# Two-layer hybrid attention trunk: in the grouped-query attention, the weight preparation of the filling matmuls is ordered behind the instructions its engines were given before it

## Chip, cores, metric

The kernel runs on one core of a Trainium2 chip. The metric is the device time of one execution in microseconds, the median of several runs.

## What is computed

A trunk of two layers (`DEPTH = 2`) over 512 latent tokens and 256 context tokens of width 1024, all in fp32. Each layer projects its normalised input once (`w_in`), runs two attentions beside each other (a neighbourhood attention, NA, and a grouped-query attention, GQA), gates each, projects each (`w_o_a`, `w_o_b`), merges them by sigmoid gates and projects the result (`w_out`). The second layer has no context queries (`update_ctx` is false there). What matters here:

```python
    b_att = _gqa_latent(qb, k_all, v_all)      # 8 query heads of 64, 2 key heads, 768 keys
    ...
    o_a = (a_att * jax.nn.silu(a_z)) @ w_o_a   # w_o_a: 512 x 1024
    o_b = (b_att * jax.nn.silu(b_z)) @ w_o_b
    merged = jax.nn.sigmoid(g_a) * o_a + jax.nn.sigmoid(g_b) * o_b
    return merged @ w_out
```

`g_a` and `g_b` are columns of the input projection (1024 each). Their matmuls, and those of `o_a`, do not depend on the GQA and are used to fill TensorE while the attention's softmax runs on the other engines.

## The kernel before

**Weights.** Every large projection is three passes of a matmul on numbers that are split into a high and a low part. `load_w2` brings a chunk of weights, 256 columns, as tiles of 128x512: SyncE issues a DMA into `raw`, ScalarE casts it (`whi`, line 420), and VectorE or GpSimd, tile by tile in turn (`mix_lo`), subtracts (`wlo = raw - whi`, line 422). `raw` has three buffers; `whi` and `wlo` have eight each, which is two chunks of four tiles. A chunk of the gates has four tiles, a chunk of `w_o_a` two.

**Stages of a layer.** Input projection, NA heads, query and key preparation of the GQA, then 8 GQA heads, then merge and output projection. In the GQA stage a list `fill` holds, alternately, the loading of a chunk and the pieces (groups of matmuls) that use a chunk. `in_order` builds it: the loads of the first two chunks, then for each chunk its pieces, followed by the load of the chunk two places further on.

```python
            fill = in_order(gates[n_na:] + o_chunks("a", prepare, evac_a))
            run(fill, 2)
```

So `run(fill, 2)` gives the loads of chunks 0 and 1. Chunks 0 to 4 are what is left of the gates (called A0 to A4 here) and four chunks of `w_o_a` follow (O0 to O3). Some pieces are given ahead of the heads (four in layer 0, two in layer 1); `pipeline` spreads the rest of the list over the 8 heads: first the scores of head h, then the values of head h-1, then a few entries of `fill`. The pieces write one PSUM buffer `psf` (lines 435 to 437, one line a pass); ScalarE empties it for the gates (`zt`, line 625), VectorE for `w_o_a` (`tg`, line 703). Ahead of the first piece of O0 stands `prepare`: `hilo` splits the gated NA output, four casts on ScalarE (`gah`, line 667) and four subtractions on GpSimd (`gal`, line 668).

**A head.** Four times: scores on TensorE into one of two PSUM buffers (`pss`, lines 886 and 887), maximum on VectorE (line 1157), exponential on ScalarE (line 1158, `p`), cast of `p` to half precision on ScalarE (`h`, line 837), its low part on VectorE or GpSimd (line 838), and a transposing DMA. The next head's query is split by a cast (line 879) and a subtraction on VectorE (`qs`, line 880). The values come a head later: a small matmul that brings the sums' reciprocals in place (line 849), the products (lines 1174 and 1175), and `ho` on ScalarE and VectorE (lines 824 and 825). In layer 0 each head also has its context queries (lines 899 to 921).

**What sets the order.** A scheduler with a simulated timeline puts the instructions of each engine into order; the order in which the code gives them counts only where a dependency says so. `behind(engine, fn, after)` adds such dependencies: it calls `fn` and ties what `fn` gives to `engine` in a row behind the instructions `after`. They are program order on that one engine and not a wait on a semaphore. `latest(engine, n)` names the last n instructions given to an engine so far.

Of the kernel before, what the change touches and what calls it, by code (L numbers as in the profile page):

```python
# [38 lines left out]
ON_PE, ON_DVE = mybir.EngineType.PE, mybir.EngineType.DVE  # L39
ON_ACT, ON_POOL, ON_SP = mybir.EngineType.Activation, mybir.EngineType.Pool, mybir.EngineType.SP  # L40
# [32 lines left out]
def hybrid_kernel(es: ExitStack, tc, x, ctx, cvec, w_ada, w_ada0, small, gvec, w_in, w_o_a, w_o_b, w_out,  # L73
# [17 lines left out]
    def big(name):  # L91
        return bigp.tile([128, 3072], F32, tag="big", name=nm(name))
# [319 lines left out]
    def load_w2(src, col0, nk, lo_eng):  # L412

        res = []
        for i in range(nk // 2):
            raw = raw_tile()
            nc.sync.dma_start(raw.rearrange("p (k n) -> p k n", k=2),
                              src[256 * i:256 * i + 256, col0:col0 + 256].rearrange("(k p) n -> p k n", k=2))
            hi = wp.tile([128, 512], F32R, tag="whi", name=nm("whi"), bufs=8)
            S.copy(hi, raw)  # L420
            lo = wp.tile([128, 512], F32R, tag="wlo", name=nm("wlo"), bufs=8)
            lo_eng(i).tensor_tensor(lo, raw, F(hi), ALU.subtract)  # L422
            res += [(hi[:, c:c + 256], lo[:, c:c + 256]) for c in (0, 256)]
        return res
# [27 lines left out]
    def chan_proj(w, f, a, n0, n1, evac, late=0):  # L452


        ps = psw(n1 - n0)
        nk = len(w)
        wh = lambda k, i: w[k][i][:, 128 * f:128 * f + 128]
        act = lambda k, i: R(a(i, k)[:, n0:n1])
        for k in range(late):
            T.matmul(ps, wh(k, 0), act(k, 0), start=k == 0, stop=False)  # L460
            T.matmul(ps, wh(k, 1), act(k, 0), start=False, stop=False)
        for k in range(late):
            T.matmul(ps, wh(k, 0), act(k, 1), start=False, stop=False)
        for k in range(late, nk):
            mm3(ps, (wh(k, 0), wh(k, 1)), (act(k, 0), act(k, 1)), k == 0, k == nk - 1)
        evac(f, n0, n1, ps)
# [3 lines left out]
    def latest(engine, n):  # L470
        return [i.name for i in nc.cur_bb.bb.instructions if i.engine == engine][-n:]

    def behind(engine, fn, after=None):

        n = len(nc.cur_bb.bb.instructions)
        after = latest(engine, 1) if after is None else after
        fn()
        for i in nc.cur_bb.bb.instructions[n:]:
            if i.engine == engine:
                for last in after:  # L480
                    tc.add_manual_dep(i, last, mybir.DependencyInfo(
                        mybir.DependencyClass.NoSync, mybir.DependencyReason.DATA), reason="program order")
                after = [i.name]
# [6 lines left out]
    def run(fill, n):  # L490
        for _ in range(min(n, len(fill))):
            fill.pop(0)()
# [102 lines left out]
    def layer(l, hx, nxt, start):  # L595
# [22 lines left out]
        def fill_chunks(col0, dst, spill, silu, eng):  # L618

            def evac(f, n0, n1, ps):  # L620
                if spill is None:
                    d = dst().rearrange("p (f n) -> p f n", f=4)[:, f, n0:n1]
                else:
                    d = ztp.tile([128, 512], F32, tag="zt", name=nm("zt"))[:, :n1 - n0]
                S.activation(d, ps, AF.Tanh, scale=0.5)  # L625
                if silu:
                    V.scalar_tensor_tensor(d, d, 1.0, ps, ALU.add, ALU.mult)
                if spill is not None:
                    (nc.sync if not first else G if silu else S).dma_start(spill[:, f, n0:n1], d)
            res = []  # L630
            for i in range(2):
                st = {}

                def ld(i=i, st=st):
                    st["w"] = load_w2(W, col0 + 256 * i, KT, eng)
                res.append((ld, [lambda f=f, n0=n0, n1=n1, i=i, st=st:
                                 chan_proj(st["w"], f, a_hx, n0, n1, lambda f, a, b, ps: evac(2 * i + f, a, b, ps))
                                 for f in range(2) for n0, n1 in spans]))
            return res

        def in_order(chunks):

            res = [ld for ld, _ in chunks[:2]]
            for i, (_, pieces) in enumerate(chunks):
                res += pieces
                if i + 2 < len(chunks):
                    res.append(chunks[i + 2][0])
            return res

        tg = [None] * 4  # L650
        n_na = GATES[l]
# [21 lines left out]
        def o_chunks(br, prepare, evac):  # L673

            src = (w_o_a if br == "a" else w_o_b)[l]
            act = lambda part, k: gated[br][part][:, k, :]
            res = []
            for i in range(4):
                st = {}

                def ld(i=i, st=st):
                    st["w"] = load_w2(src, 256 * i, 4, pool_lo if br == "b" and i == 0 else mix_lo)
                pieces = [lambda f=f, n0=n0, n1=n1, i=i, st=st:
                          chan_proj(st["w"], f, act, n0, n1, lambda f, a, b, ps: evac(2 * i + f, a, b, ps),
                                    3 if br == "b" and i == 0 and first else 0)
                          for f in range(2) for n0, n1 in spans]
                res.append((ld, ([prepare] if i == 0 and prepare else []) + pieces))
            return res
# [80 lines left out]
        fill = fill_chunks(C_AZ, lambda: za, None, True, mix_lo) + fill_chunks(C_BZ, None, zs, True, mix_lo)  # L769
        gates = []  # L770
        for c in range(4):
            gates += g_chunks(c)
        fill = in_order(fill + gates[:n_na])
        run(fill, 2)
        for t in range(qt):
# [11 lines left out]
        if True:  # L787
# [326 lines left out]
                run(bg, 1)  # L1114
            hp["lag"] = 2
            qbv = big("qb").rearrange("p (j n) -> p j n", j=4)
            fill = in_order(gates[n_na:] + o_chunks("a", prepare, evac_a))
            run(fill, 2)

            def evac_bq(t, ps):  # L1120
# [83 lines left out]
        with tc.tile_pool(name=f"mrg{l}", bufs=1, reuse_waits="tile") as mp:  # L1204
# [16 lines left out]
            chunks = o_chunks("b", None, evac_b)  # L1221
# [223 lines left out]
    def nxt():  # L1445
        if not hx1:
            hx1.extend([[big("hx") for _ in range(2)] for _ in range(2)])
        return hx1
    layer(0, hx0, nxt, start)
    layer(1, hx1, None, None)  # L1450


# [73 lines left out]
```

## Time and profile before

| | |
|---|---|
| time, median of 3 runs | 1111.2 us (1111.06 to 1111.54) |
| the profiled execution | 1110.55 us, span 1108.8 us |
| mean granted clock of TensorE | 0.995 |
| TensorE matmul busy | 1074.5 us (97%) |
| VectorE busy | 767.4 us (69%) |
| ScalarE busy | 617.2 us (56%) |
| GpSimd busy | 470.1 us (42%) |

Times in the profile are from the start of the span. The GQA stage of layer 0 lies at about 375 to 530 us, that of layer 1 at about 920 to 1040 us. In the rows, a number in brackets at the end is the idle time of the engine just before the instruction, with what ended it. PE is TensorE, DVE VectorE, ACT ScalarE, POOL GpSimd, SPq the DMA queue of SyncE.

### The profile page before, as it was taken

The numbers are of one execution on the slowest core, as the hardware profiler recorded it, in microseconds if no ns is written. First come the engines' busy times: TensorE is split into PE (matmuls) and PEld (weight loads), VectorE is DVE, ScalarE is ACT, GpSimd is POOL, SyncE is SP. The second block draws the span as 40 slices with busy tenths as digits, with TensorE's granted clock in tenths as the row PEclk, the third lists the DMA queues.
The fourth block names the chain that finished last, engine by engine and source line by source line (L and its number), as shares of the span: only waits on it lengthen the run. The fifth ranks groups of instructions, "written<-read, shape, count | busy, mean of one in ns | idle before, by whom it ended". The sixth has DMA issues, their size and how long they took to land. (4 is left out here: it accounts for less than half of the span.)

```text
span 1108.8 us, 16943 instructions
## 1 busy us (share of the span) xinstructions
PE 1074.5 (97%) x5672; PEld 876.9 (79%) x5672; DVE 767.4 (69%) x1600; ACT 617.2 (56%) x1236; POOL 470.1 (42%) x397
## 2 busy tenths in 40 slices
PE   8999999899999999979999999999999999999998
PEld 6688888788888877757788878888877888777677
DVE  5567799974378478676577785466997665777473
ACT  6464279776333566655330275444899446786430
POOL 1044235554256244454521455232355472564531
PEclk9999999999999999989999999999999999999999
DMA  9454325554543498769533542453565536879642
GB/s 374 153 169 143 91 70 116 125 137 121 174 141 117 132 205 185 172 185 271 171 105 125 166 136 82 138 165 99 132 148 130 156 106 171 200 232 236 188 152 77
DMA packets 236001, 171.79 MB, mean 155 GB/s; under 512 B 160141, under 2 KB 201865, under 8 KB 234249
## 3 DMA queue, kind: packets, MB, share of 16 engines
q1 hardware_dynamic: 228576, 156.31, 51.7%
q0 software_dynamic: 2368, 7.87, 2.2%
q10 hardware_dynamic: 4968, 6.53, 1.8%
q8 instruction: 45, 0.74, 0.3%
q14 instruction: 44, 0.35, 0.1%
HBM read 115.58 MB, written 17.32 MB: 120 GB/s over the span
## 5 line engine op out<-in xcount | busy, mean ns | idle before, releaser
L838 POOL TENSOR_TENSOR h<-p,h 128x256 f16<-128x256 f32 (+2 forms) x104 | 113.1, 1096 | 167.7 <-ACT h L837 119.9
L422 POOL TENSOR_TENSOR wlo<-raw,whi 128x512 fp32r<-128x512 f32 x70 | 98.8, 1416 | 124.5 <-ACT whi L420 80.9
L435 PE MATMUL psf<-hx,whi 128*128 128x512 f32 (+1 forms) x360 | 137.5, 382 | 2.5 <-ACT zt L625 1.3
L437 PE MATMUL psf<-hx,wlo 128*128 128x512 f32 (+1 forms) x360 | 135.5, 376 | 0.0
L436 PE MATMUL psf<-hx,whi 128*128 128x512 f32 (+1 forms) x360 | 135.4, 376 | 0.0
L435 PE MATMUL psx<-whi,hx 128*128 128x512 f32 (+1 forms) x328 | 121.0, 372 | 0.0
L420 ACT CAST whi<-raw 128x512 fp32r<-128x512 f32 x136 | 82.9, 620 | 67.5 <-DMA raw<-in_w_in_dram 48.3
L437 PE MATMUL psx<-whi,hx 128*128 128x512 f32 (+1 forms) x328 | 120.0, 367 | 0.0
L436 PE MATMUL psx<-wlo,hx 128*128 128x512 f32 (+1 forms) x328 | 119.6, 366 | 0.0
L408 POOL TENSOR_TENSOR wlo<-raw,whi 128x512 fp32r<-128x512 f32 x40 | 59.5, 1489 | 119.2 <-ACT whi L405 76.0
L405 ACT CAST whi<-raw 128x512 fp32r<-128x512 f32 x88 | 54.2, 623 | 96.8 <-PE psx L437 34.2
L508 POOL TENSOR_TENSOR ss<-ss,ehalf 128x8 f32<-128x8 f32 (+2 forms) x40 | 63.6, 1593 | 77.8 <-DVE ss L505 72.5
L422 DVE TENSOR_TENSOR wlo<-raw,whi 128x512 fp32r<-128x512 f32 x66 | 70.8, 1073 | 35.2 <-ACT whi L420 34.1
L837 ACT CAST h<-p 128x256 f16<-128x256 f32 (+2 forms) x136 | 81.6, 616 | 7.7 <-DMA ct<-h 3.7
L435 PEld LDWEIGHTS psf<-hx,whi 128*128 128x128 f32 x360 | 67.8, 188 | 15.1 <-ACT zt L625 2.5
L1157 DVE CUSTOM_DVE_ANT_0 p<-pss,vb 128x768 f32<-128x768 f32 x64 | 60.4, 954 | 25.4 <-PE pss L887 22.7
L1158 ACT ACTIVATE p<-pss,mx 128x768 f32<-128x768 f32 x64 | 57.6, 901 | 35.7 <-DVE mx L1157 34.8
L437 PEld LDWEIGHTS psf<-hx,wlo 128*128 128x128 f32 x360 | 67.8, 188 | 11.8
L436 PEld LDWEIGHTS psf<-hx,whi 128*128 128x128 f32 x360 | 67.9, 189 | 10.7
L437 PEld LDWEIGHTS psx<-whi,hx 128*128 128x128 f32 x328 | 61.9, 189 | 10.2
L436 PEld LDWEIGHTS psx<-wlo,hx 128*128 128x128 f32 x328 | 62.0, 189 | 9.4
L435 PEld LDWEIGHTS psx<-whi,hx 128*128 128x128 f32 x328 | 61.8, 189 | 9.1 <-issue 0.2
(338 smaller groups left out, 2972.4 us busy)
## 6 DMA issues: line engine op xcount, KB each, us to landing
raw<-in_w_in_dram SPq DMA_DIRECT2D x168, 256.0 KB, 2.9
rawb<-in_w_ada_dram SPq DMA_DIRECT2D x48, 256.0 KB, 2.8
raw<-in_w_out_dram SPq DMA_DIRECT2D x32, 256.0 KB, 2.9
tg<-gs SPq DMA_DIRECT2D x4, 1536.0 KB, 7.1
rawx<-in_w_ada_dram SPq DMA_DIRECT2D x4, 1024.0 KB, 10.7
rawy<-in_w_ada_dram SPq DMA_DIRECT2D x4, 1024.0 KB, 9.3
gs<-zt ACTq DMA_DIRECT2D x16, 256.0 KB, 2.9
raw<-in_w_o_a_dram SPq DMA_DIRECT2D x16, 256.0 KB, 3.1
```

Source lines behind the costliest of these rows:

```text
L405: S.copy(hi[:, :n], raw[:, :n])
L408: e.tensor_tensor(lo[:, :n], raw[:, :n], F(hi[:, :n]), ALU.subtract)
L420: S.copy(hi, raw)
L422: lo_eng(i).tensor_tensor(lo, raw, F(hi), ALU.subtract)
L435: T.matmul(ps, lhs[0], rhs[0], start=first, stop=False)
L436: T.matmul(ps, lhs[0], rhs[1], start=False, stop=False)
L437: T.matmul(ps, lhs[1], rhs[0], start=False, stop=last)
L508: G.tensor_tensor(ss, ss, ehalf[:, :n], ALU.pow)
L837: S.copy(h[:, 0], p[:, :n])
L838: eng.tensor_tensor(h[:, 1], p[:, :n], h[:, 0], ALU.subtract)
L1157: V.tensor_tensor_reduce(p, pss, lift, -1.0, 3e38, ALU.add, ALU.min, mx[:, 0:1])
L1158: S.activation(p, pss, AF.Exp, bias=mx[:, 0:1], accum_out=r[:, i:i + 1])
```

## The change

`in_order` takes a flag. Where it is set, which is only for the list `fill` of the GQA stage (of both layers), the loads of the chunks after the first two (A2, A3, A4, O0 to O3) are given through `tied`: their casts on ScalarE stand in a row behind the last four instructions given to ScalarE before them, and their subtractions on VectorE in a row behind the last four given to VectorE. Their DMAs and the subtractions on GpSimd get no such dependency. No instruction is added or removed.

```diff
-        def in_order(chunks):
+        def tied(fn):
+            behind(ON_ACT, lambda: behind(ON_DVE, fn, latest(ON_DVE, 4)), latest(ON_ACT, 4))
+
+        def in_order(chunks, tie=False):
 
             res = [ld for ld, _ in chunks[:2]]
             for i, (_, pieces) in enumerate(chunks):
                 res += pieces
                 if i + 2 < len(chunks):
-                    res.append(chunks[i + 2][0])
+                    ld = chunks[i + 2][0]
+                    res.append((lambda ld=ld: tied(ld)) if tie else ld)
             return res
...
-            fill = in_order(gates[n_na:] + o_chunks("a", prepare, evac_a))
+            fill = in_order(gates[n_na:] + o_chunks("a", prepare, evac_a), True)
             run(fill, 2)
```

What this does to the engines' rows is shown at two places. In the changed kernel the line numbers behind the edit are four higher (line 1158 is 1162 there). The numbers behind a name are those of the tiles, the same in both kernels.

The first place is the start of layer 1's heads. On ScalarE before, from the third exponential of head 0 (`p_9883`) to the second of head 1 (`p_10007`); the casts of chunk A2 (`whi_9906`, `whi_9912`, `whi_9918`, `whi_9924`) stand some 15 rows above, before head 0's first exponential:

```order
L420 CAST whi_10085<-raw_10083 128x512
L625 ACTIVATE zt_9981<-psf_9956 128x512
L879 CAST qs_10145<-qb_9536 64x512
L1158 ACTIVATE p_9883,r_2006_9851<-pss_9878,mx_9884 128x768
L837 CAST h_9887<-p_9883 128x768
L1158 ACTIVATE p_9896,r_2006_9851<-pss_9891,mx_9897 128x768
L837 CAST h_9900<-p_9896 128x768
L625 ACTIVATE zt_10114<-psf_10089 128x512
L1158 ACTIVATE p_9994,r_2041_9988<-pss_9989,mx_9995 128x768
L1158 ACTIVATE p_10007,r_2041_9988<-pss_10002,mx_10008 128x768
```

And ScalarE now:

```order
L625 ACTIVATE zt_9981<-psf_9956 128x512
L883 CAST qs_10145<-qb_9536 64x512
L1162 ACTIVATE p_9883,r_2006_9851<-pss_9878,mx_9884 128x768
L1162 ACTIVATE p_9896,r_2006_9851<-pss_9891,mx_9897 128x768
L841 CAST h_9887<-p_9883 128x768
L841 CAST h_9900<-p_9896 128x768
L420 CAST whi_9906<-raw_9904 128x512
L420 CAST whi_9912<-raw_9910 128x512
L420 CAST whi_9918<-raw_9916 128x512
L1162 ACTIVATE p_9994,r_2041_9988<-pss_9989,mx_9995 128x768
L1162 ACTIVATE p_10007,r_2041_9988<-pss_10002,mx_10008 128x768
```

Three casts of A2 have moved from ahead of head 0 to the end of it, and the fourth comes still later; the cast `whi_10085`, of chunk A3, has left this place too.

On TensorE, in the same place before, the last score of head 0 (`pss_9891`) is followed by the 24 matmuls of A2's first piece (`psf_10089`), of which the first six are:

```order
L887 MATMUL pss_9891<-gk_9240,qs_9847 128x256
L435 MATMUL psf_10089<-hx_6680,whi_9906 128x512
L436 MATMUL psf_10089<-hx_6682,whi_9906 128x512
L437 MATMUL psf_10089<-hx_6680,wlo_9908 128x512
L435 MATMUL psf_10089<-hx_6680,whi_9906 128x512
L436 MATMUL psf_10089<-hx_6682,whi_9906 128x512
L437 MATMUL psf_10089<-hx_6680,wlo_9908 128x512
```

And TensorE now, from the second score of head 1 (`pss_10002`):

```order
L890 MATMUL pss_10002<-gk_9240,qs_9984 128x512
L891 MATMUL pss_10002<-gk_9240,qs_9984 128x512
L890 MATMUL pss_10002<-gk_9240,qs_9984 128x256
L891 MATMUL pss_10002<-gk_9240,qs_9984 128x256
L853 MATMUL pst_10041<-ident,r_2006_9851 128x128 x4
L435 MATMUL psf_10089<-hx_6680,whi_9906 128x512
L436 MATMUL psf_10089<-hx_6682,whi_9906 128x512
L890 MATMUL pss_10015<-gk_9240,qs_9984 128x512
L891 MATMUL pss_10015<-gk_9240,qs_9984 128x512
L890 MATMUL pss_10015<-gk_9240,qs_9984 128x256
L891 MATMUL pss_10015<-gk_9240,qs_9984 128x256
L437 MATMUL psf_10089<-hx_6680,wlo_9908 128x512
```

The piece has moved behind the first two scores of head 1 (`pss_9989`, `pss_10002`) and the small matmul of head 0's divisor (`pst_10041`), and the third score (`pss_10015`) cuts it after two matmuls.

The second place is in layer 0, where `prepare` runs. On VectorE before, around the low part of the second tile of chunk O1 (`wlo_5499`):

```order
L1157 ISA p_5553,mx_5554<-pss_5548,vb_3419 128x768
L1157 ISA mx_5554 128x1
L850 SCALAR_TENSOR_TENSOR zb_4067<-pst_5616,vb_3419,zb_4067 64x512
L422 TENSOR_TENSOR wlo_5499<-raw_5495,whi_5497 128x512
L880 TENSOR_TENSOR qs_5721<-qb_3734,qs_5721 64x768
L847 RECIPROCAL r_5431<-r_5431 128x2
L825 TENSOR_TENSOR ho_5471<-psv_5462,ho_5471 64x256
```

And VectorE now:

```order
L1161 ISA p_5553,mx_5554<-pss_5548,vb_3419 128x768
L1161 ISA mx_5554 128x1
L854 SCALAR_TENSOR_TENSOR zb_4067<-pst_5616,vb_3419,zb_4067 64x512
L884 TENSOR_TENSOR qs_5721<-qb_3734,qs_5721 64x768
L851 RECIPROCAL r_5431<-r_5431 128x2
L829 TENSOR_TENSOR ho_5471<-psv_5462,ho_5471 64x256
```

`wlo_5499` has left the row and comes some time later; the split of the next head's query (`qs_5721`) takes its place, and the rest of the row is as before.

On GpSimd before, in the same stretch, where `gal_5309` is the four subtractions of `prepare`, `wlo_5493` the first tile of O1 and `wlo_5671` the first of O2:

```order
L829 TENSOR_TENSOR zb_4067<-zb_4067,ho_5458 64x512
L422 TENSOR_TENSOR wlo_5493<-raw_5489,whi_5491 128x512
L668 TENSOR_TENSOR gal_5309<-za_1053,gah_5308 128x768 x4
L422 TENSOR_TENSOR wlo_5671<-raw_5667,whi_5669 128x512
L829 TENSOR_TENSOR zb_4067<-zb_4067,ho_5471 64x256
```

And GpSimd now:

```order
L833 TENSOR_TENSOR zb_4067<-zb_4067,ho_5458 64x512
L672 TENSOR_TENSOR gal_5309<-za_1053,gah_5308 128x768 x4
L833 TENSOR_TENSOR zb_4067<-zb_4067,ho_5471 64x256
L842 TENSOR_TENSOR h_5434<-p_5430,h_5434 128x512
L422 TENSOR_TENSOR wlo_5493<-raw_5489,whi_5491 128x512
```

The four subtractions of `prepare` now stand between two additions to `zb`, and the low parts of O1 and O2 that stood around them come later.

## Prediction

> **What bounds the kernel now.** I read the page first, then the busy time by stage, then the waits of the matmul engine stage by stage, then the timeline around its longest wait.
>
> ```profile
> span 1108.8 us, 16943 instructions
> PE 1074.5 (97%) x5672; PEld 876.9 (79%) x5672; DVE 767.4 (69%) x1600; ACT 617.2 (56%) x1236; POOL 470.1 (42%) x397
> ```
>
> TensorE is busy for 97% of the span, so no other engine's work is the bound as such. The change adds no work; it can only open or close holes on TensorE, or change its clock. The busy time in the layer-0 heads, the layer-1 heads and the rest (columns: length, then busy time and instruction count for PE, PEld, DVE, ACT and POOL, then granted clock) shows where holes are:
>
> ```profile
> 375.00:530.00 155.00, 141.33 (x786) 113.36 (x784) 111.04 (x198) 101.04 (x195) 72.25 (x51) 0.97 0.81 196
> 920.00:1040.00 120.00, 116.60 (x550) 88.74 (x550) 81.43 (x130) 83.70 (x150) 64.70 (x43) 1.00 0.86 213
> ```
>
> The heads of layer 0 have 155.00 - 141.33 = 13.7 us of idle TensorE and a clock under 1; those of layer 1 have only 3.4 us. The waits of TensorE name them (the first two rows are of layer 0's window, the third of layer 1's):
>
> ```profile
> PE psv L849 <- DVE ho L825: 5.8, 1, 5.8
> PE psf L435 <- ACT zt L625: 2.0, 2, 1.6
> PE psf L436 <- POOL gbl L668: 1.1, 1, 1.1
> ```
>
> So there is one large hole in layer 0 to win, and in layer 1 a stage that is nearly full, where a cast that comes late can only cost.
>
> **Part 1: layer 0, where `prepare` runs.** The hole in detail:
>
> ```profile
> 482.17 1.14 ACT L420 CAST whi<-raw 128x512 fp32r<-128x512 f32 x2
> 483.33 0.38 ACT L625 ACTIVATE zt<-psf 128x256 f32<-128x256 f32 x1
> 483.76 0.49 PE L435 MATMUL psf<-gah,whi 128*128 128x512 f32 x1 [1.60 <-ACT zt L625]
> 484.84 0.79 PE L436 MATMUL psf<-gal,whi 128*128 128x512 f32 x1 [0.58 <-POOL gal L668]
> 493.56 0.69 PE L849 MATMUL psv<-ident,r 128*128 128x128 f32 x2 [5.79 <-DVE ho L825]
> ...
> 481.75 1.27 POOL L422 TENSOR_TENSOR wlo<-raw,whi 128x512 fp32r<-128x512 f32 x1
> 482.98 7.12 POOL L668 TENSOR_TENSOR gal<-za,gah 128x768 fp32r<-128x768 f32 x4
> 490.05 1.27 POOL L422 TENSOR_TENSOR wlo<-raw,whi 128x512 fp32r<-128x512 f32 x1
> ...
> 483.66 8.22 DVE L422 TENSOR_TENSOR wlo<-raw,whi 128x512 fp32r<-128x512 f32 x1
> 491.91 0.95 DVE L880 TENSOR_TENSOR qs<-qb,qs 64x768 fp32r<-64x768 f32 x1
> 492.89 0.17 DVE L847 RECIPROCAL r<-r 128x2 f32<-128x2 f32 x1
> 493.09 0.42 DVE L825 TENSOR_TENSOR ho<-psv,ho 64x256 f32<-64x256 f32 x1
> ```
>
> VectorE's subtraction `wlo_5499` starts at 483.66, while GpSimd runs the four `gal` and then another `wlo` without a break, and ends at 491.88, 0.56 us after GpSimd's last. Behind it on VectorE stand the split of the query, the reciprocal and `ho`, and TensorE waits for that `ho`. The clock falls too (granted clock is the third column from the end):
>
> ```profile
> 484.00:488.00 4.00, 3.18 (x8) 2.15 (x7) 4.00 (x1) 3.92 (x10) 4.00 (x3) 0.59 1.07 421
> 492.00:496.00 4.00, 2.44 (x8) 2.15 (x9) 3.13 (x5) 0.00 (x0) 1.84 (x2) 0.50 0.08 18
> 496.00:500.00 4.00, 4.00 (x15) 2.85 (x15) 2.44 (x5) 1.82 (x3) 0.37 (x1) 0.71 0.68 163
> ```
>
> In the last of these windows half rate holds for (1 - 0.71) x 2 x 4.00 = 2.3 us, so until about 498.3; from 493.56 on, 4.7 us run at half rate and some 2.4 us are lost to it. Price of the whole incident: 1.60 + 0.58 + 5.79 + 2.4 = 10.4 us.
>
> What the change removes here: the two casts at 482.17, so `zt` at 483.33 can follow the matmuls at once and the 1.60 hole nearly goes; the `wlo` of GpSimd at 481.75, so `gal` starts 1.23 us sooner; the `wlo` behind `gal`; and `wlo_5499` itself. What stays: the split of the query, which also reads two operands from SBUF, now arrives at VectorE at 483.66, in the middle of `gal`. I take it that it is held as `wlo_5499` was: until 482.98 + 7.12 - 1.23 = 488.87, plus the 0.56 above and its follow-up (0.17 + 0.42 and the gaps, 493.56 - 492.86 = 0.70), which puts the matmul of line 849 at about 490.4 instead of 493.56. The hole on TensorE is still there, so the half clock is too. Gain 3.1 us. Bounds: 1.2 us if VectorE is held as much longer as before, 10.4 less 0.9 (the query's own 0.95) = 9.5 us if it is not held at all.
>
> **Part 2: layer 1, start of the heads.** Here the move costs:
>
> ```profile
> 931.14 0.62 ACT L420 CAST whi<-raw 128x512 fp32r<-128x512 f32 x1 [0.86 <-DMA raw<-in_w_in_dram]
> 932.66 0.90 ACT L1158 ACTIVATE p<-pss,mx 128x768 f32<-128x768 f32 x1
> 933.46 0.19 ACT L1158 ACTIVATION_READ_ACCUMULATOR p<-pss,mx 128x1 f32 x1
> 935.44 0.83 ACT L837 CAST h<-p 128x768 f16<-128x768 f32 x1
> ...
> 936.35 1.65 POOL L838 TENSOR_TENSOR h<-p,h 128x768 f16<-128x768 f32 x1 [3.50 <-ACT h L837]
> ...
> 931.25 0.96 DVE L1157 CUSTOM_DVE_ANT_0 p<-pss,vb 128x768 f32<-128x768 f32 x1 [1.16 <-PE pss L887]
> ...
> 931.64 0.28 PE L887 MATMUL pss<-gk,qs 128*128 128x256 f32 x1
> 932.31 0.50 PE L435 MATMUL psf<-hx,whi 128*128 128x512 f32 x1 [0.39 <-ACT zt L625]
> 937.89 0.39 PE L886 MATMUL pss<-gk,qs 128*128 128x512 f32 x1
> 938.60 0.39 PE L886 MATMUL pss<-gk,qs 128*128 128x512 f32 x1
> 939.30 0.60 PE L849 MATMUL pst<-ident,r 128*128 128x128 f32 x4
> ```
>
> Before, TensorE filled 932.31 to 937.89 (5.58 us, 24 matmuls of A2's first piece), while ScalarE did head 0's last exponentials and casts. Now the piece's casts come behind all of that. Step by step:
>
> - The maximum at 931.25 ends at 932.21, so `p_9883` runs 932.25 to 933.3 (0.90 and the sum's 0.19), some 0.4 us sooner than before, as the cast at 931.14 is gone from ScalarE. Both score buffers are full until then: `pss_9989` starts at 933.3, TensorE idle from 931.92.
> - `p_9896` ends at 934.35; then `pss_10002` (one score is 938.60 - 937.89 = 0.71) until 935.06, and the divisor's matmul, about 0.35.
> - The two casts `h` (0.83 each) end at 936.0 and `whi_9906` (0.62) at 936.6: two matmuls, then TensorE waits again. `whi_9912` and `whi_9918` (0.57 each by the row at 482.17) go ahead of `p_9994`, which ends at 938.8; then `pss_10015` runs until 939.5. The piece's low part `wlo_9908` on GpSimd, behind the 1.65 of `h_9900` and with some 1.3 of its own (the row at 481.75), is there by 939.0.
> - At 939.5 there remain 22 of the 24 matmuls, 5.1 us, so this stretch of work ends at 944.6. Before, all but the 0.71 of `pss_10015` was done at 939.65: 940.35. Loss 4.2 us. Bounds 3.5 (if `zt` and the query's cast let ScalarE start sooner) and 4.8 (if the exponential starts at 932.66 as before).
>
> TensorE has about 2.2 us of work in the 6.9 us to 938.8 (two scores, the divisor's, two of the piece). In layer 0 a stretch so thin brought half clock: the row 484 to 488 has 0.59, that is 4.00 x (1 - 0.59) = 1.64 us lost. I add 1.7 for one such stretch here; bounds 0 and 3.3 (two). [...]
>
> Nothing makes this up later: the whole stage has 3.4 us of idle TensorE, in pieces of other causes. SyncE's queue also changes: the load of A2's fourth tile and of two tiles of A3 now stand between the transposes of head 0 and head 1, waiting for `raw` buffers that the late low parts free at about 940; head 1's transposes come after that anyway (its first exponential ends at 938.8). Cost nothing; cover gone would be about 1 us on the values of head 1, a head later.
>
> **Part 3: everywhere else.** In layer 0 the same shift hits a start of the heads where the context queries and a finished piece stand in between; by the casts' durations (4 x 0.62) against that cover I count 0, at most 0.7. Later chunks arrive one head later and are used one head later: 0. At the end of layer 1 casts of `w_o_b`'s part stand ahead of the last exponentials; of before's holes there (1.1 in the row above) one may close, and up to three casts and three `gbh` may delay the last values (about 6 x 0.57 less cover = 2.7): I take +0.5.
>
> **Sum.** -3.1 + 4.2 + 1.7 + 0.5 = +3.3 us on the profiled 1110.55: 1113.85. The median of the runs, 1111.2, is 0.65 above the profiled run, so 1114.5.
>
> **Rivals.** *VectorE slips in between (faster).* In layer 1 the same four subtractions hold VectorE only for one of them:
>
> ```profile
> 984.31 5.63 POOL L668 TENSOR_TENSOR gal<-za,gah 128x512 fp32r<-128x512 f32 x4 [0.51 <-ACT gah L667]
> 987.38 1.42 DVE L422 TENSOR_TENSOR wlo<-raw,whi 128x512 fp32r<-128x512 f32 x1
> ```
>
> If the query's split gets in so, `ho` is there before TensorE asks for it, the clock stays full, and part 1 gains 9.5: -9.5 + 4.2 + 1.7 + 0.5 = -3.1, or 1108.1 as a median. It decides from a wait of under 2 us at 483.66. Against it: 8.22 us over four `gal`, in this very place. [...] Chance 0.25.
>
> *No thin stretch (no change).* The clock in layer 1 stays full and the tail is even: -3.1 + 4.2 = +1.1, 1112.3. For it: the stretch still has some matmuls in it every 2 us. Chance 0.17.
>
> *The hole of layer 0 stays (slower, more).* GpSimd's row behind `gal` keeps VectorE out as long as before, and the gain is 1.2 at most; with two slow stretches in layer 1: -1.2 + 4.2 + 3.3 + 0.5 = +6.8, 1118.0. For it: VectorE got in only when GpSimd's whole row had run out. Chance 0.15.
>
> That the change moves nothing is excluded by the order of the instructions, which differs at both places.
>
> **How the numbers follow.** The forecast has the rest, 0.43: 1114.5, its own range 1112 to 1117. A measurement of this kernel can tell about 0.2%, 2.2 us, from no change, so up to 1113.4 is the same: some 0.08 of the forecast and 0.14 of the second rival, 0.22. Slower: 0.35 of the forecast, 0.15 and 0.03: 0.53. Faster: 0.25. The range takes in the first rival with 1.1 us to spare and the last with 1.5: 1107.0 to 1119.5.
>
> **What would show it.** Right: in layer 0 the wait of line 853 (849 before) for `ho` shrinks to about 2.5 to 3.5 us, with the split of the query at about 6 us in place of the 8.22; in layer 1 waits on `p` and `whi` of together about 4.5 us between 931 and 940, and a clock under 1 right after. Wrong: no long VectorE instruction beside `gal` (first rival), a clock of 1.00 from 936 to 944 (second), or VectorE held past 491 (third); or waits over 1 us at places that part 3 counts at 0.

## The result and the profile after

| | before | after |
|---|---|---|
| median | 1111.2 us (5 runs, 1109.65 to 1111.54) | 1124.44 us (5 runs, 1123.44 to 1127.78) |
| ratio | | 1.0127, 95% interval 1.0115 to 1.0139 |
| profiled execution, span | 1110.55, 1108.8 us | 1125.78, 1123.9 us |

The change makes the kernel 1.3% slower, 13 us, outside the range that was given. The traces compared below differ by 15.1 us of span, some 2 us more than the medians. The head of the page after:

```profile
span 1123.9 us, 16910 instructions
PE 1078.6 (96%) x5672; PEld 880.5 (78%) x5672; DVE 769.5 (68%) x1600; ACT 617.3 (55%) x1236; POOL 466.2 (41%) x397
```

The same 5672 matmuls take 4.1 us longer (1078.6 to 1074.5; the mean granted clock is 0.989 after and 0.995 before), and TensorE idles 45.3 us instead of 34.3. Of the 15.1 us of span, 11.0 are holes and 4.1 slower matmuls. Where in the program they arise is read from the same work's start in the two traces. Two pairs of rows, before and after each: the first transposes of layer 1's input (line 343, the same in both kernels) and the first scores of layer 1's NA heads (line 974, after 978); the two times are the first and the last start:

```profile
L343 PE MATMUL pst<-ident,y x48: 270/272/327, 639.2 to 672.1; 128*128 128x128 f32 x48
L974 PE MATMUL pss<-kh,qs x24: 387/392/481, 775.2 to 847.6; 128*128 128x512 f32 x24
```

```profile
L343 PE MATMUL pst<-ident,y x48: 269/273/330, 646.6 to 687.8; 128*128 128x128 f32 x48
L978 PE MATMUL pss<-kh,qs x24: 386/392/480, 787.3 to 859.3; 128*128 128x512 f32 x24
```

By the first transposes of layer 1, where layer 0 ends, the changed kernel is 7.4 us late; by the NA heads of layer 1 it is 12.1. The last score of GQA head 0 in layer 1 ends at 931.92 before and 943.75 after, 11.8 late, and the span's end is 15.1 late: the GQA stage of layer 1 and what follows cost only 3.3.

Layer 0's GQA stage, before and after (columns as in the prediction: length, busy time of PE, PEld, DVE, ACT, POOL, then granted clock):

```profile
480.00:504.00 24.00, 15.98 (x72) 11.86 (x70) 19.20 (x21) 12.62 (x25) 14.81 (x11) 0.79 0.76 242
504.00:550.00 46.00, 44.10 (x242) 34.18 (x243) 27.45 (x46) 21.16 (x42) 25.66 (x19) 1.00 0.76 191
```

```profile
480.00:504.00 24.00, 15.65 (x72) 11.27 (x71) 19.84 (x22) 12.51 (x24) 13.66 (x10) 0.79 0.77 237
504.00:550.00 46.00, 37.57 (x188) 29.63 (x187) 24.57 (x40) 18.89 (x38) 24.10 (x19) 0.89 0.86 221
```

The stretch with `prepare` is as bad as before; nothing was won there. The stretch behind it, which the prediction counted at nothing, lost 6.5 us of TensorE's busy time (44.10 to 37.57), and what ran there ran at a clock of 0.89.

The hole at `prepare`, after; TensorE, VectorE and GpSimd:

```profile
482.55 0.50 PE L436 MATMUL psf<-gal,whi 128*128 128x512 f32 x1 [0.89 <-POOL gal L672]
488.92 0.79 PE L890 MATMUL pss<-gk,qs 128*128 128x512 f32 x1 [5.42 <-ACT p L909]
491.16 0.69 PE L853 MATMUL psv<-ident,r 128*128 128x128 f32 x2 [0.59 <-DVE ho L829]
497.23 0.50 PE L890 MATMUL pss<-gk,qs 128*128 128x512 f32 x1 [1.42 <-ACT p L1162]
...
480.27 7.54 DVE L905 TENSOR_SCALAR mx<-mx 128x2 f32<-128x2 f32 x1
489.50 0.95 DVE L884 TENSOR_TENSOR qs<-qb,qs 64x768 fp32r<-64x768 f32 x1
...
480.69 7.10 POOL L672 TENSOR_TENSOR gal<-za,gah 128x768 fp32r<-128x768 f32 x4
```

The held instruction is neither a low part nor the query's split. It is the addition of a constant to a maximum of 128x2 numbers (line 905), which takes 0.15 to 0.38 us at its seven other places and 7.54 here, to the end of the four `gal`. It stands ahead of the next score's maximum, so TensorE stops at a score, 4 us sooner than before. A sign of this stood in the trace of before, at the same instruction, and the prediction passed over it (the GpSimd addition to `zb` beside it ran from 480.50 to 481.79, so both ended nearly together):

```profile
481.32 0.56 DVE L901 TENSOR_SCALAR mx<-mx 128x2 f32<-128x2 f32 x1
```

The holes behind it, after, and SyncE's queue at that place, before and after:

```profile
512.41 0.38 PE L1178 MATMUL pst<-ht,vb 128*128 128x512 f16 x1 [2.31 <-issue]
521.55 0.65 PE L853 MATMUL pst<-ident,r 128*128 128x128 f32 x4 [1.83 <-DVE r L851]
540.08 0.58 PE L435 MATMUL psf<-gah,whi 128*128 128x256 f32 x1 [3.21 <-DVE tg L707]
...
537.47 1.83 DVE L422 TENSOR_TENSOR wlo<-raw,whi 128x512 fp32r<-128x512 f32 x1 [1.68 <-ACT whi L420]
```

```profile
498.35 0.96 SPq L671 DMA_DIRECT2D tg<-gs  x2
499.75 6.02 SPq L842 DMA_TRANSPOSE ct<-h  x1
```

```profile
498.53 0.47 SPq L675 DMA_DIRECT2D tg<-gs  x1
499.86 10.32 SPq L846 DMA_TRANSPOSE ht<-h  x3
512.73 0.71 SPq L675 DMA_DIRECT2D tg<-gs  x1
```

Loads of `tg` of 1.5 MB stand before the transposes of a head's probabilities in both kernels. After, the products of a head (line 1178) come 13 us behind the last head's (499.47 and 512.41), as fewer of `w_o_a`'s pieces stand between; before, 21 us (499.27 and 520.51). The row at 512.41 names no releaser, but the view of the transposed tiles `ht` from 496 to 516 does: TensorE's matmul waits 2.3 us for them, and they take up to 9.6 us from issue to landing (minimum, median and maximum below; before, 3.3, 3.8 and 4.2, with no wait of TensorE):

```profile
PE pst L1178: 2.3, 1
DMA to landing us min/median/max: 3.6/8.0/9.6
```

The largest hole, 3.21 at 540.08, is of another kind. TensorE waits for `tg`, the emptying of `psf` on VectorE, and this stands behind the low part at 537.47, which waited for its cast and then ran 1.83 us beside GpSimd's `gbl`.

Layer 1's start, after, is close to the prediction's walk: waits for `p`, `whi`, `p` and `wlo` of 1.60, 0.57, 1.20 and 0.43, and then a clock of 0.57:

```profile
945.35 0.50 PE L890 MATMUL pss<-gk,qs 128*128 128x512 f32 x1 [1.60 <-ACT p L1162]
948.20 0.50 PE L435 MATMUL psf<-hx,whi 128*128 128x512 f32 x1 [0.57 <-ACT whi L420]
950.13 0.49 PE L890 MATMUL pss<-gk,qs 128*128 128x512 f32 x1 [1.20 <-ACT p L1162]
951.52 0.50 PE L437 MATMUL psf<-hx,wlo 128*128 128x512 f32 x1 [0.43 <-POOL wlo L422]
...
952.00:956.00 4.00, 4.00 (x13) 3.09 (x12) 2.64 (x4) 2.19 (x5) 3.04 (x2) 0.57 1.25 256
```

### The profile page after: what moved, and what is told of

The parts are those of the page before. It is cut to its first block, busy times and chain, and to the rows that moved or that the text cites. A ratio compares the mean times of both kernels' runs of the same rounds, so it can differ in the third digit from the quotient of the medians.

```text
span 1123.9 us, 16910 instructions
## 1 busy us (share of the span) xinstructions
PE 1078.6 (96%) x5672; PEld 880.5 (78%) x5672; DVE 769.5 (68%) x1600; ACT 617.3 (55%) x1236; POOL 466.2 (41%) x397
## 5 line engine op out<-in xcount | busy, mean ns | idle before, releaser
L422 POOL TENSOR_TENSOR wlo<-raw,whi 128x512 fp32r<-128x512 f32 x70 | 100.5, 1443 | 105.3 <-ACT whi L420 65.0
L408 POOL TENSOR_TENSOR wlo<-raw,whi 128x512 fp32r<-128x512 f32 x40 | 53.3, 1335 | 132.5 <-ACT whi L405 93.8
L422 DVE TENSOR_TENSOR wlo<-raw,whi 128x512 fp32r<-128x512 f32 x66 | 61.7, 935 | 29.1 <-ACT whi L420 28.9
```

The source lines that it names most:

```text
L408: e.tensor_tensor(lo[:, :n], raw[:, :n], F(hi[:, :n]), ALU.subtract)
```

## The experiments

Theory A was formed on the trace after: layer 0 carries most of the loss, by a held VectorE row that isn't shortened and by filling work that comes late behind it; layer 1 loses its start only. The rivals stand in each expectation. All ratios below are to the kernel before on the same chip; medians of different tables can come from different chips, so kernels are best compared by their ratios. A diff is against the changed kernel unless another is named.

### Which layer, which engine

```diff
-            fill = in_order(gates[n_na:] + o_chunks("a", prepare, evac_a), True)
+            fill = in_order(gates[n_na:] + o_chunks("a", prepare, evac_a), first)      # l0_only
+            fill = in_order(gates[n_na:] + o_chunks("a", prepare, evac_a), not first)  # l1_only
...
-            behind(ON_ACT, lambda: behind(ON_DVE, fn, latest(ON_DVE, 4)), latest(ON_ACT, 4))
+            behind(ON_ACT, fn, latest(ON_ACT, 4))                                      # act_only
+            behind(ON_DVE, fn, latest(ON_DVE, 4))                                      # dve_only
```

> The tie is kept in layer 0 alone. Theory A, from the trace of the changed kernel: layer 0 carries most of the loss, about 8 us by the end of its heads and some 4 more at the start of layer 1, and layer 1's heads only 3 to 4: this kernel takes 1119 to 1124 us. Rival (the prediction's reckoning): layer 0 gains 1 to 3 us and the loss is layer 1's: 1108 to 1112 us.

> The tie is kept in layer 1 alone. Theory A: the start of the layer-1 heads loses 4.2 us of waits and 1.7 us of half clock, less up to 2 us that later holes give back: 1114 to 1117.5 us. Rival (the loss of the changed kernel is layer 1's): above 1120 us.

> Only ScalarE's casts are tied, in both layers; VectorE's low parts are free. Theory A: a low part can't come ahead of its cast, so tying the casts does it all: within 2 us of the changed kernel, 1122 to 1127 us. Rival: the places on VectorE matter by themselves, and half of the loss or more goes: 1112 to 1118 us.

> Only VectorE's low parts are tied, in both layers; the casts are free. Theory A: the casts stand where they stood, but every second tile's low part still comes late, so a piece starts and stops after its first tile: 1113 to 1119 us. Rival: the low parts carry the whole loss: 1122 us or more.

| kernel | median us | ratio, 95% interval |
|---|---|---|
| l0_only | 1119.28 | 1.0072 (1.0056 to 1.0087) |
| l1_only | 1113.90 | 1.0024 (1.0012 to 1.0035) |
| act_only | 1124.47 | 1.0113 (1.0098 to 1.0128) |
| dve_only | 1116.76 (1111.74 to 1123.70) | 1.0066 (1.0043 to 1.0089) |

Layer 0 alone loses 8 us and layer 1 alone 2.6, so the prediction had the two layers the wrong way round. Tying the casts alone costs as much as the whole change, as theory A expected: a low part can't come ahead of its cast. Tying the low parts alone also costs, but its runs scatter over 12 us, and the one trace is of its fastest. `l1_only` ends just under theory A's 1114.

Layer 1 alone, at the start of the heads and in the rest of its GQA stage; then the four waits again, and the 4 us behind the third of them:

```profile
920.00:960.00 40.00, 35.70 (x167) 27.21 (x166) 24.64 (x42) 28.67 (x51) 17.01 (x10) 1.00 0.75 159
960.00:1050.00 90.00, 87.13 (x413) 65.37 (x411) 61.41 (x94) 60.47 (x106) 55.11 (x36) 1.00 0.92 236
...
934.61 0.50 PE L890 MATMUL pss<-gk,qs 128*128 128x512 f32 x1 [1.60 <-ACT p L1162]
937.47 0.50 PE L435 MATMUL psf<-hx,whi 128*128 128x512 f32 x1 [0.57 <-ACT whi L420]
939.40 0.50 PE L890 MATMUL pss<-gk,qs 128*128 128x512 f32 x1 [1.20 <-ACT p L1162]
940.78 0.50 PE L437 MATMUL psf<-hx,wlo 128*128 128x512 f32 x1 [0.41 <-POOL wlo L422]
...
940.00:944.00 4.00, 3.59 (x17) 2.86 (x16) 2.38 (x3) 3.18 (x7) 4.00 (x3) 1.00 1.09 162
```

The waits are the same to a hundredth or two, but the clock is 1.00 where the changed kernel had 0.57. The same thin stretch costs 1.7 us of clock in one kernel and nothing in the other.

### Which chunks

```diff
-                    res.append((lambda ld=ld: tied(ld)) if tie else ld)
+                    res.append((lambda ld=ld: tied(ld)) if tie and i + 2 < 5 else ld)         # l0_gates: A2 to A4
+                    res.append((lambda ld=ld: tied(ld)) if tie and i + 2 >= 5 else ld)        # l0_o: O0 to O3
+                    res.append((lambda ld=ld: tied(ld)) if tie and i + 2 in (7, 8) else ld)   # l0_o23: O2, O3
+                    res.append((lambda ld=ld: tied(ld)) if tie and i > 0 else ld)             # l1_from3: all but A2
+                    res.append((lambda ld=ld: tied(ld)) if tie and i == 0 else ld)            # l1_a2: A2 alone
```

The first three tie layer 0 alone (`tie` is `first` there), the last two layer 1 alone (`not first`).

> Layer 0 alone, and only the gate chunks A2 to A4 tied; O0 to O3 are free. Theory A: the loss of layer 0 has two parts, the held VectorE row beside the four subtractions of GpSimd (no gain from the move, about 0) and weights that come a head later at the end of the stage (some 8 us); the second comes with the tied chunks O0 to O3, so here little is lost: 1110 to 1114 us. Rival: every chunk's delay hands itself on to the next, so the gates alone cost as much as all: 1118 us or more.

> Layer 0 alone, and only O0 to O3 tied. Theory A: the end of the stage is late as in the changed kernel: 1116 to 1121 us. Rival: the loss comes from the gate chunks: 1109 to 1113 us.

> Layer 0 alone tied, and only the last two chunks O2 and O3. Theory A: the low part of O2 still leaves the row behind gal, the held instruction stays where it was before, and what these chunks' lateness costs at the end of the stage shows by itself: 1112 to 1116 us. Rival (the late end of the stage is the larger part of O0 to O3's loss): 1117 us or more; or O0 and O1 carry it all: 1110 to 1111.5 us.

> Layer 1 alone tied, with A2 free: A2's weights are ready ahead of the heads as before. Theory A: layer 1's loss is A2's piece at the start of the heads, so nothing is lost: 1109 to 1112 us, no wait of over 0.6 us between 925 and 945. Rival (every tied chunk of the layer costs its share): 1113 us or more.

> Layer 1 alone, and only A2 tied. Theory A (the prediction's part 2): A2's piece behind head 0's exponentials costs 4 us of waits and 1.7 us of clock, a little of which later holes give back: 1113 to 1117 us, with waits on p and whi of 3 to 4.5 us at the start of the heads. Rival (one free or tied chunk between others makes the loss, by ScalarE's zt standing behind casts): 1110 to 1112 us.

| kernel | median us | ratio, 95% interval |
|---|---|---|
| l0_gates | 1110.20 | 0.9992 (0.9982 to 1.0003) |
| l0_o | 1121.20 | 1.0090 (1.0075 to 1.0105) |
| l0_o23 | 1124.53 | 1.0111 (1.0078 to 1.0145) |
| l1_from3 | 1115.52 | 1.0037 (1.0024 to 1.0051) |
| l1_a2 | 1122.95 | 1.0111 (1.0094 to 1.0128) |

In layer 0 the gate chunks cost nothing, and the last two chunks of `w_o_a` alone cost as much as all (theory A had put `l0_o23` at 1112 to 1116): of the chunks that the prediction called one head later and free, the gates were free and O0 to O3 were not.

How O0 to O3 cost it is not the same in every kernel. In `l0_o` no matmul waits over 0.4 us for a transpose between 504 and 550. Its largest hole there is again a wait for `tg`, behind a low part on VectorE that took 5.85 us beside four instructions of GpSimd and ended 0.55 us after the last of them; VectorE, GpSimd and TensorE:

```profile
528.93 5.85 DVE L422 TENSOR_TENSOR wlo<-raw,whi 128x512 fp32r<-128x512 f32 x1
535.34 0.69 DVE L707 SCALAR_TENSOR_TENSOR tg<-tg,psf 128x512 f32<-128x512 f32 x1
...
529.02 2.77 POOL L842 TENSOR_TENSOR h<-p,h 128x768 f16<-128x768 f32 x2
531.75 2.48 POOL L422 TENSOR_TENSOR wlo<-raw,whi 128x512 fp32r<-128x512 f32 x2
...
536.08 0.58 PE L435 MATMUL psf<-gah,whi 128*128 128x256 f32 x1 [4.00 <-DVE tg L707]
```

And `l0_o` starts the first transposes of layer 1 at 641.4, only 2.2 us behind the kernel before, but the NA heads at 786.1, 10.9 behind: most of its lateness shows between these two places.

In layer 1 theory A holds for the start of the heads and fails for the sum. With A2 free the waits at the start are gone, but others come further on, where ScalarE's `zt` stands late, and the kernel is slower than theory A's 1109 to 1112 (l1_from3):

```profile
953.19 0.50 PE L435 MATMUL psf<-hx,whi 128*128 128x512 f32 x1 [2.18 <-ACT zt L625]
966.83 0.50 PE L435 MATMUL psf<-hx,whi 128*128 128x512 f32 x1 [2.01 <-ACT zt L625]
```

With A2 alone tied the start's waits are there (1.60, 0.57, 1.20), and behind them come further waits for exponentials, up to 4.0 us, in a stage where the changed kernel has few; the list of waits of l1_a2, third number the longest:

```profile
PE pss L890 <- ACT p L1162: 9.5, 5, 4.0
```

From 960 to 1050 TensorE is busy for 81.24 us at a clock of 0.96 there, where `l1_only` has 87.13 at 1.00. So a tie on one chunk changes where the scheduler puts everything that follows, and the loss of a part is not a part of the loss. Why A2 alone costs more than all of layer 1's chunks together is not settled.

### The held row

```diff
-            hilo(za, gated["a"], range(4))
+            hilo(za, gated["a"], range(4), V if first else G)   # before_galv (in the kernel before), after_galv, and each l0_..galv..
...
-                    V.tensor_scalar(mx, mx, P_LOG, None, ALU.add)
+                    for i in range(2):                          # mx1
+                        V.tensor_scalar(mx[:, i:i + 1], mx[:, i:i + 1], P_LOG, None, ALU.add)
```

> The kernel before, with layer 0's four subtractions gal on VectorE instead of GpSimd (same result). Theory A: they hold VectorE for 7 to 8 us and with TensorE's waits and half clock cost some 10 us; on VectorE they take 4 x 0.96 us: 1101 to 1106 us. Rival (TensorE waits there for something else, the casts or the context's exponentials): within 3 us of before, 1108 to 1114 us.

> The changed kernel with the same move of gal to VectorE in layer 0. Theory A: the held row goes here too, the late weights stay: 1113 to 1118 us, 10 to 14 us above before with the same move. Rival (the late weights only cost because of the long hole ahead of them): within 6 us of before with the same move.

> The changed kernel with the context maximum's 128x2 addition (line 905) on VectorE cut into two of 128x1; every engine's row is otherwise in the same order. Theory A: only the 128x2 form is held by GpSimd, two of 128x1 take about 0.1 to 0.2 us each beside gal; the held instruction is then the query's split, as the prediction had it, and VectorE has served the maxima ahead of it: 3 to 8 us under the changed kernel, 1116 to 1121 us, with the longest VectorE instruction at line 885 (the query's split) and 5 to 7 us. Rival (any addition to SBUF tiles is held, whatever its shape): same time as the changed kernel, 1123 to 1126 us, one of the two additions held 7 us.

> Layer 0 alone tied, and its four gal on VectorE. Theory A: the changed kernel with gal on VectorE (1106.2 us) less layer 1's loss of 2.6 us: 1102 to 1105 us, below both kernels. Rival (the layers' losses depend on each other): 1106 us or more.

| kernel | median us | ratio, 95% interval |
|---|---|---|
| before_galv | 1112.87 | 1.0014 (1.0003 to 1.0026) |
| after_galv | 1106.16 | 0.9958 (0.9944 to 0.9973) |
| mx1 | 1123.04 | 1.0100 (1.0077 to 1.0122) |
| l0_galv | 1104.18 | 0.9929 (0.9913 to 0.9946) |

`mx1` is the cleanest of them, for the rows of VectorE and GpSimd around `gal` keep their order. VectorE, GpSimd and TensorE in it, and the sixteen halves of the addition in the whole trace (minimum, median and maximum in ns):

```profile
481.25 0.21 DVE L906 TENSOR_SCALAR mx<-mx 128x1 f32<-128x1 f32 x2
483.59 6.05 DVE L884 TENSOR_TENSOR qs<-qb,qs 64x768 fp32r<-64x768 f32 x1
...
480.44 1.28 POOL L833 TENSOR_TENSOR zb<-zb,ho 64x512 f32<-64x512 f32 x1
481.68 7.14 POOL L672 TENSOR_TENSOR gal<-za,gah 128x768 fp32r<-128x768 f32 x4
...
490.34 0.69 PE L853 MATMUL psv<-ident,r 128*128 128x128 f32 x2 [5.14 <-DVE ho L829]
...
L906 DVE TENSOR_SCALAR mx<-mx x16: 135/144/156, 388.6 to 524.1; 128x1 f32<-128x1 f32 x16
```

Cut in two, the addition takes 0.21 us for both, in the middle of GpSimd's addition to `zb` (480.44 to 481.72). The single addition on 128x2 numbers stood at the same place in the kernel before and lasted 0.56 us there, to the end of that instruction (481.88 and 481.79). So the form decides here: two of 128x1 were not held where one of 128x2 was. Then the query's split is held from 483.59, for 6.05 us, and the divisor's matmul starts at 490.34, as the prediction had it ("at about 490.4"). TensorE comes to this place sooner, though, so its wait is 5.14 us and not the 2.5 to 3.5 that were forecast, and the waits of the stretch sum to 7.1 us where the changed kernel has 8.3. The median falls by 1.4 us, with intervals that overlap, and not by the 3 to 8 us of theory A: TensorE still idles 6.8 us between 504 and 550.

Moving `gal` to VectorE takes the holding beside `gal` away: in `after_galv` the addition takes 0.17 us at 486.78 and the query's split 0.95 behind it. In the changed kernel this gives 18 us, from 1124.4 to 1106.2, more than theory A expected; in the kernel before it gives nothing and costs 1.6 (theory A had 5 to 10 us there, and was wrong). The two stretches, in the kernel before and then in the changed kernel, both with the move:

```profile
480.00:504.00 24.00, 19.86 (x98) 15.27 (x98) 18.65 (x27) 14.59 (x27) 10.78 (x7) 0.86 0.94 274
504.00:550.00 46.00, 41.70 (x230) 32.72 (x229) 25.90 (x44) 21.30 (x42) 24.49 (x19) 0.96 0.81 183
...
480.00:504.00 24.00, 21.25 (x120) 16.13 (x119) 20.75 (x32) 15.39 (x31) 10.53 (x8) 1.00 1.00 273
504.00:550.00 46.00, 41.42 (x230) 32.88 (x229) 27.49 (x47) 20.38 (x39) 25.27 (x18) 1.00 0.78 217
```

In the kernel before, the move wins 3.9 us of TensorE's time at `prepare` and loses 2.4 behind it (44.10 to 41.70). In the changed kernel it wins in both stretches, 5.6 and 3.9 us. With the move the tie of layer 0 is a gain: `l0_galv`, tied in layer 0 alone, is the fastest kernel, 0.7% under the one before, as theory A expected.

### What was still open: the holes between 505 and 548

```diff
                 for c in (1, 3):
                     tg[c] = big("tg")
-                    load_tg(c)
+                    if first:                                            # after_tglate, before_tglate, l0_galv_tglate
+                        behind(ON_SP, lambda: load_tg(c), latest(ON_SP, 2))
+                    else:
+                        load_tg(c)
                 gated["b"] = hilo_tiles("gb")
-                hilo(zb, gated["b"], range(3))
+                hilo(zb, gated["b"], range(3), V if first else G)        # l0_galv_gblv alone
```

> The changed kernel with layer 0's last two loads of tg (1.5 MB each, at 498.5 and 512.7 us) given behind the last head's transposes on SyncE's queue. Theory A: these loads keep the transposes of the heads waiting (7 to 9 us instead of 1.4 to 4) and TensorE with them, now that less filling work stands between the values of two heads: 1116 to 1120 us. Rival (the loss is the late weights and the held VectorE rows, transposes only wait with them): 1122 to 1126 us.

> The kernel before with the same move of the two loads. Theory A: before, filling work covered the late transposes, so nothing changes: 1109 to 1113 us. Rival (the loads cost in any order): 1104 to 1108 us.

> Layer 0 alone, only the gate chunks tied, gal on VectorE. Theory A (without the held row the ties of O0 to O3 cost nothing, or gain by keeping casts out of the way of zt): within 3 us of the same kernel with all chunks tied, 1102 to 1108 us. Rival (the ties of O0 to O3 are what gains once gal is on VectorE): 1108 us or more, near the kernel before with gal on VectorE.

> Layer 0 alone tied, gal and also the three gbl of the end of the stage on VectorE. Theory A: the second held row (a low part of 1.9 us instead of 0.7 beside gbl, then a wait of TensorE of 1.5 us for tg) goes: 1101 to 1104 us. Rival (three times 0.96 us on VectorE at the end of the stage delays tg and zb as much): 1104 us or more.

> Layer 0 alone tied, gal on VectorE, and the last two loads of tg behind the last transposes. Theory A: with gal on VectorE the transposes land in time anyway, so the late loads only cost what they cost the kernel before (4 us): 1106 to 1110 us. Rival (the two causes are separate and add up): 1098 to 1102 us.

| kernel | median us | ratio, 95% interval |
|---|---|---|
| after_tglate | 1119.96 | 1.0093 (1.0075 to 1.0110) |
| before_tglate | 1114.55 | 1.0043 (1.0026 to 1.0059) |
| l0_gates_galv | 1111.41 | 1.0013 (1.0001 to 1.0026) |
| l0_galv_gblv | 1113.11 | 1.0018 (1.0003 to 1.0033) |
| l0_galv_tglate | 1111.84 | 1.0011 (0.9995 to 1.0026) |

With the two loads behind the last transposes, the changed kernel's stretch reads

```profile
504.00:550.00 46.00, 44.97 (x261) 36.40 (x260) 31.92 (x56) 22.79 (x46) 26.29 (x20) 1.00 0.84 257
```

instead of 37.57 at a clock of 0.89: the holes are gone, with the ties left as they are. So in the changed kernel late filling work costs there because of these loads: without them in front, three transposes of `ht` take the queue 6.09 us from 500.73 on, where the changed kernel's three took 10.32 from 499.86 on, and TensorE idles 1.03 us in the whole stretch instead of 8.43. The hole at `tg` is gone too, which the transposes alone don't explain; the move also gives VectorE's row another order. The profiled run starts layer 1's first transposes at 636.6, 10.0 us before the changed kernel and 2.6 before the one before, and keeps 10.0 to the NA heads (777.3). It gives back 3.8 in the rest of layer 1, where the edit changes nothing, so that the median falls by only 4.5 us; why is open. Moved so, the loads cost the kernel before some 4 us (neither theory A nor the rival had that) and `l0_galv` 7.7. That the gains of the two moves add up is refuted.

`l0_gates_galv` shows that, with `gal` on VectorE, the gain hangs on the ties of O0 to O3, the same ties that cost layer 0's whole loss with `gal` on GpSimd: its rival was right. `gbl` on VectorE as well was expected to win 0 to 3 us and lost 9. Both are facts without a settled reason: each of these kernels is also a new schedule.

## Why the prediction was wrong

- **Sign and direction.** Slower was the likeliest, and it is slower; 13 us against the 3.3 of the sum, beyond the last rival (1118.0). The sign of the sum came from part 2, and the stage and its end in layer 1 cost 3.3 us; most of the loss lies in layer 0 and between the layers, where the sum had a gain and nothing. That the sign came out is in part luck.
- **Part 3, "Later chunks arrive one head later and are used one head later: 0": this is the step that failed.** It is true for the gates (`l0_gates`, 0.9992) and false for O0 to O3 (`l0_o`, 1.0090, +10 us). In its place the runs showed 6.5 us of TensorE's time lost between 504 and 550. What was overlooked is what filling work covers: not only softmax, but the transposes behind 1.5 MB loads on SyncE's queue, and the time for which a low part keeps `tg` waiting on VectorE. `after_tglate` shows the first: with the loads out of the way the stretch has 44.97 us of work again. The second is read from the traces (3.21 us in the changed kernel, 4.00 in `l0_o`) and was not tried by itself. The trace of before had both a load and the transpose of 6.02 us behind it, and the 21 us of cover between two heads' products.
- **Part 1, -3.1 us: measured about 0.** The step "the split of the query ... now arrives at VectorE at 483.66" took the row ahead of it to be free to pass. It was held 3.4 us sooner, at the context's maximum. The four waits at this place sum to 8.3 us (0.89, 5.42, 0.59 and 1.42), those of before to 8.0. `mx1` shows the step as it was meant, at 490.34 (the terms that the prediction names sum to 490.1; the rest up to 490.4 is the query's split being longer than the low part). The first rival's mechanism, VectorE let in after one `gal`, did not occur in layer 0; the third, held as long as before, is what came nearest. The price of 10.4 us for the whole incident leaves out the 1.64 us lost in the row 484 to 488 at its clock of 0.59, and it is no forecast of what its removal brings: `before_galv` takes the holding away and gains nothing.
- **Between the layers, not priced at all: +4.7 us** (from 7.4 at the first transposes to 12.1 at the NA heads). TensorE has 1.6 us of waits for line 408's low parts there that before had not; the rest is not accounted for. This stretch takes 136 us in the kernel before, `l0_gates`, `after_galv` and `l0_galv`, 141 in the changed kernel and `after_tglate`, and 145 in `l0_o` and `act_only`. It is 141 in `before_tglate` too, which ties nothing, so the ties alone don't set it, and moving the loads doesn't mend it. No run was made for this; it stays open.
- **Part 2, +4.2 us and 1.7 of clock: right as a mechanism.** The four waits sum to 3.8 us, and the loss at a clock of 0.57 behind them to 4.00 x (1 - 0.57) = 1.7 us in the changed kernel, 0 in `l1_only`. The waits appear in every trace in which A2's casts are tied in layer 1 and are not in `l1_from3`, where A2 is free. The stage and its end together cost 3.3 us where the sum had 6.4 with the +0.5 for the end; of the 5.5 at the start, some 2 us came back later in the layer.
- **The clock.** The same waits were followed by 0.57 in one kernel and by 1.00 in another, so the clock cannot be priced from the length of a hole alone. No hole at this place is over 1.60 us in either, and no run moves the waits alone, so what made the difference was not shown.

## What to carry to other kernels

Work that fills an engine can cover more than the wait one looks at (here transposes that took up to 9.6 us to land, for which TensorE waited 2.3 us once the cover was thinner): before making it later, list every transfer that lands under it, with its size and what stands behind it on its queue. VectorE's row was held here by an addition on 128x2 numbers, 7.54 us for an instruction of 0.15 to 0.38 us elsewhere in the same trace, so walk the row from the start of the blocking stretch and not from the instruction that was held last time. When a scheduler places the rest, measure the parts of a change and don't add them up: here layer 0's tie gave +8.0 us, the move of `gal` +1.6, and both together -7.6.

## What the runs showed of the hardware

An addition of VectorE on 128x2 numbers took 7.54 us in the changed kernel, beside four subtractions of GpSimd, and 0.17 us in `after_galv`, where these run on VectorE. It was held at two places in the kernel before too, to the end of what GpSimd ran: it took 1.42 us at 443.69, to 445.11, and GpSimd's subtraction ended at 445.07; and 0.56 us at 481.32, to 481.88, with GpSimd's addition to `zb` ending at 481.79. Two additions on 128x1 numbers did the same work in `mx1`: the sixteen of them took 0.14 to 0.16 us each, and the two at 481.25 took 0.21 us together, in the middle of GpSimd's addition to `zb` (480.44 to 481.72).

At four places VectorE was kept out over a row of GpSimd's instructions, three to five of them, and let in only when the row ran out: 8.22 us before, 7.54 after, 6.05 in `mx1`, 5.85 in `l0_o`. In layer 1 the row at 987.38 that the prediction shows was let in sooner, for it ended at 988.80 and GpSimd's four ran on to 989.94; what makes the difference was not tried.
